# A mixture-of-experts layer: gate/up of two experts in four passes, and TensorE's order fixed to the program's

## Chip, cores, metric

One core of a Trainium2 chip runs the whole layer in one launch. The metric is the device time of one execution in microseconds. A core has TensorE (matmuls), VectorE, ScalarE, GpSimd and SyncE; SyncE issues the weight loads, and 16 DMA engines carry them.

## What is computed

A layer on 512 tokens of width 1024, all in float32: a mixer (mLSTM heads and pooling), then a mixture of 32 experts of which each token takes four, each time with a residual, and a last norm. The change lies in the experts:

```python
logits = xt @ w_router + b_router
top_vals, top_idx = lax.top_k(logits, 4)
top_gates = softmax(top_vals)
# for each expert e, on the tokens that chose it:
gate = minimum(xb @ w_gate[e] + b_gate[e], 7.0)
up = clip(xb @ w_up[e] + b_up[e], -7.0, 7.0)
y = (gate * sigmoid(1.702 * gate) * (up + 1.0)) @ w_down[e] + b_down[e]
# out[token] += top_gate * y
```

The three matrices of an expert are 1024 x 1024 floats, 4 MB each; the 32 experts have 384 MB together, and each is read once.

## The kernel before

The mixer and the router take the first 230 us or so; after them come the experts, which this document calls the expert stage.

**Tokens and blocks.** The tokens of an expert are gathered in blocks of 32, by GpSimd's indirect DMAs. A block is computed in four column quarters on the four 32-row groups of TensorE, so that gate and up of a block fill one PSUM bank (`gub[b]`, 128 x 512) and its down projection half a bank (`db[b]`; blocks 2 and 3 use `gub[2:]` for it). Each expert has room for four blocks. Blocks 0 and 1 are always computed, block 2 under `If(CR[e] > 64)` and block 3 in a second If inside it, `If(CR[e] > 96)`, on the count of tokens that TensorE reads into a register. Here expert 0 has three blocks, expert 1 and expert 2 two each; experts 29, 30 and 31 have three; two experts (9 and 25) have four; the others two or three. Where an If is not taken, TensorE jumps over its matmuls.

**Weights.** Gate and up of an expert come in four chunks of 2.1 MB (two DMAs, a quarter of gate and a quarter of up), down in two chunks of the same size (one DMA each): `load_chunks`, L121 to L145. A chunk goes into one of ten slots in turn (in the trace `wr`, `ym`, `wlo`, `whi`, by the buffer that the space came from). The order is gate/up of experts 0 and 1, down of 0, gate/up of 2, down of 1, gate/up of 3, and so on; so gate/up of expert 2 takes over the slots of gate/up of expert 0, down of 1 and the first half of gate/up of 3 those of expert 1, the second half of gate/up of 3 those of down of 0, and down of 2 and the first half of gate/up of 4 those of gate/up of 2. SyncE issues the loads in this order, each once the slot's last reader is through; eight DMAs can be under way.

**The work on a chunk.** `gu_mm` (L916 to L925) multiplies blocks by chunks; `each` (L891 to L903) cuts an expert's eight row groups into passes: in each pass blocks 0 and 1 over the pass's chunks, then block 2 under its If, then block 3. `GU_STEPS` gives the number of passes of an expert's gate/up: two for experts 0 and 1, four for 30 and 31, one for the others; down always has one pass, over both chunks (`d_mm`, L958 to L970). Ahead of each gate/up two small matmuls put the bias into `gb` (L912, called at L1133), ahead of each down projection into `yb`. VectorE takes gate/up out of PSUM (`act_blocks`, first at L931), ScalarE has the sigmoid, VectorE the products and the transposes for the down projection. Behind expert 0's gate/up the softmax of the gates runs (`softmax`, matmuls at L999).

**The order.** In the loop over `g["way"]` (L1123 on) the program writes the work expert by expert, but a scheduler may reorder each engine's instructions where dependencies allow. It also moves whole Ifs. `tc.manual_schedule` on an engine keeps the order of the program: before, for TensorE in expert 0's gate/up alone (`ME = (0,)`), and for four engines (`ENDM`) behind expert 30's down projection to the end.

Of the kernel before, what the change touches and what calls it, by code (L numbers as in the profile page):

```python
# [14 lines left out]
AF = mybir.ActivationFunctionType  # L15
# [9 lines left out]
NE = 32  # L25
# [12 lines left out]
RD = 2  # L38
ENDM = ("PE", "DVE", "Activation", "Pool")
HA = (False, False)  # L40
GU_STEPS = {0: 2, 1: 2, 30: 4, 31: 4, NE: 1}
D_STEPS = {NE: 1}
DBG = {}
CA = 2
PB = 2
MAN = ()
ME = (0,)


@with_exitstack  # L50
def tile_block(ctx, tc, x, norm1_g, w_in, ig_b, fg_b, conv_w, head_norm_g, pool_w, pool_scale,
# [111 lines left out]
    open_ring(RING, "right")  # L163
    mixer(tc, nc, ctx, g)
    moe(tc, nc, ctx, g)
    overflow(tc, nc, ctx, g)

# [670 lines left out]
def moe(tc, nc, ctx, g):  # L838
    pe, act, dve, gp, sp = nc.tensor, nc.scalar, nc.vector, nc.gpsimd, nc.sync
# [7 lines left out]
    with tc.tile_pool(name="mo", bufs=1) as mo, tc.tile_pool(name="mop", bufs=1, space=PSUM) as pp:  # L847
        gub = [pp.tile([128, 512], F32, name=f"gub{b}") for b in range(NB)]
        db = [pp.tile([128, 512], F32, name=f"db{b}") for b in range(2)] + gub[2:]
        gb = pp.tile([128, 512], F32, name="gb")  # L850
        yb = pp.tile([128, 512], F32, name="yb")[:, :256]
        gbs = mo.tile([128, 512], F32, name="gbs")
# [10 lines left out]
        def gather(e, between=None):  # L863
            gather_block(e, 0)
            i = gather_block(e, 1)
            if between:
                between()
            with tc.issue_after(i.ins):
                GR[e] = gp.value_load(cnt[0:1, e:e + 1], min_val=0, max_val=S)
            with tc.If(GR[e] > 64):  # L870
                gather_block(e, 2)
                with tc.If(GR[e] > 96):
                    gather_block(e, 3)
            if e == 0:
                g["rest"][0](1)

        def select(e):
            SEL[e] = mo.tile([128, 128], FR, name="sel", tag="sel", bufs=2)
            act.activation(SEL[e].rearrange("p (q i) -> p q i", q=4),
                           ident[:, 4 * e:4 * e + 4, None].to_broadcast([128, 4, 32]), AF.Copy)  # L880

        def xpose(e):
            XT[e] = []
            for b in range(NB):
                t = mo.tile([128, 256], F32, name=f"xt{b}", tag=f"xt{b}", bufs=2) if b < 3 else xgt[:, 4]
                i = dve.transpose(t, xg[b])  # L886
                if b:
                    tc.keep_in_program_order(i)
                XT[e].append(t)

        def each(e, mm, steps):  # L891

            for i in range(steps):
                cs = range(8 * i // steps, 8 * (i + 1) // steps)
                if e == NE - 1 and i == steps - 1:
                    for b in (2, 0, 1, 3):
                        some(e, mm, b, cs)
                    continue
                mm(e, (0, 1), cs)
                with tc.If(CR[e] > 64):  # L900
                    mm(e, (2,), cs)
                    with tc.If(CR[e] > 96):  # L902
                        mm(e, (3,), cs)  # L903

        def some(e, mm, b, cs):
            with tc.If(CR[e] > 32 * b) if b > 1 else ExitStack():
                mm(e, (b,), cs)

        def bias(e, ps, c0, c1, alone=True):
            with tc.issue_after(last[0]) if last and alone else ExitStack():  # L910
                for part in range(2):
                    i = pe.matmul(ps, SEL[e], par[:, part, c0:c1], start=(part == 0), stop=(part == 1 and alone))  # L912
            if not last:
                last[:] = [i.ins]
# [57 lines left out]
        def y_block(e, b):  # L972
            y = mo.tile([128, 256], F32, name="y", tag="sy", bufs=6)
            if e < NE - 1:
                dve.tensor_tensor(y, db[b][:, :256], ybs, op=OP.add)  # L975
            dve.tensor_scalar(y, y if e < NE - 1 else db[b][:, :256], gs[:, e * NB + b:e * NB + b + 1], None,  # L976
                              op0=OP.mult)
            return y
# [24 lines left out]
        def scatter_block(e, b, y):  # L1003
            i = gp.indirect_dma_start(out=yd, out_offset=bass.IndirectOffsetOnAxis(  # L1004
                ap=gi[:, e * NB + b:e * NB + b + 1], axis=0), in_=y, in_offset=None,
                bounds_check=S * 4 - 1, oob_is_err=False, compute_op=OP.add)
            for o in scat[4 * e:]:
                tc.declare_no_dep(i.ins, o.ins, reason="an expert's tokens differ")
            scat.append(i)

        def for_blocks(e, f):
            f(0)
            f(1)
            with tc.If(GR[e] > 64):
                f(2)
                with tc.If(GR[e] > 96):  # L1016
                    f(3)

        def finish_early():

            a, t2 = g["ring_tile"](), g["ring_tile"]()
            t2 = t2.rearrange("p a b -> p (a b)")
            nfb, nfq, yg, junk = t2[:, 0:1024], t2[:, 1024:1280], t2[:, 1280:2304], t2[:, 2304:3328]
            nf = g["normf_g"]
            act.dma_start(nfb, nf.partition_broadcast(128))
            for q in range(4):
                act.dma_start(nfq[q * 32:(q + 1) * 32, :], nf[q * 256:(q + 1) * 256].partition_broadcast(32))
            gp.memset(yg, 0.0)  # L1028

            quarters, qi = t2[:, 3328:3456], t2[:, 3456:3584].bitcast(I32)  # L1030
            gp.iota(qi, pattern=[[1, 128]], base=128, channel_multiplier=-1)
            dve.tensor_scalar(qi, qi, 31, None, op0=OP.bitwise_and)
            dve.tensor_scalar(quarters, qi, 0.0, None, op0=OP.is_equal)
            e = NE - 1

            def fetch(b):
                gp.indirect_dma_start(out=yg[:, b * 256:(b + 1) * 256], out_offset=None, in_=yd,  # L1037
                                      in_offset=bass.IndirectOffsetOnAxis(ap=gi[:, e * NB + b:e * NB + b + 1], axis=0),
                                      bounds_check=S * 4 - 1, oob_is_err=False)

            for_blocks(e, fetch)
            for t in range(NT):
                if t == RD:
                    g["final"][0](1)
                read(a, t)
            if RD == NT:
                g["final"][0](1)
            return dict(a=a, nfb=nfb, yg=yg, nfq=nfq, junk=junk, quarters=quarters, sums=t2[:, 3584:3600])

        def read(a, t):  # L1050
            sp.dma_start(a[:, t], yd[t * 512:(t + 1) * 512, :].rearrange("(p j) w -> p (j w)", j=4))
# [54 lines left out]
                todo[step[0]](int(step[1]))  # L1106

        CR, last = {}, []
        if MAN:
            ctx.enter_context(tc.manual_schedule(engines={getattr(mybir.EngineType, n) for n in MAN}))  # L1110
        def begin():
            for ps in gub[2:]:
                dve.memset(ps, 0.0)
# [5 lines left out]
        act.activation(gbs, gb, AF.Copy)  # L1119
        xpose(0)  # L1120
        g["order"].close()
        final = {}
        for kind, e in g["way"]:  # L1123
            if kind == "gu":
                with tc.issue_after(last[0]):
                    CR[e] = pe.value_load(cnt[0:1, e:e + 1], min_val=0, max_val=S)
                if e + 1 < NE:
                    gather(e + 1)
                    select(e + 1)
                    xpose(e + 1)  # L1130
                with tc.manual_schedule(engines={mybir.EngineType.PE}) if e in ME else ExitStack():
                    if e:
                        bias(e, gb, 0, 512)  # L1133
                        act.activation(gbs, gb, AF.Copy)  # L1134
                    each(e, gu_mm, GU_STEPS.get(e, GU_STEPS[NE]))
                load_chunks(4)
                if e == 0:
                    softmax()
                act_blocks(e)
                continue  # L1140
            if e < NE - 1:
                bias(e, yb, 512, 768)
                act.activation(ybs, yb, AF.Copy)
            if e < NE - 1:
                each(e, d_mm, D_STEPS.get(e, D_STEPS[NE]))
            load_chunks(2)
            if e < NE - 1:
                ys = [y_block(e, b) for b in range(NB)]
                for_blocks(e, lambda b: scatter_block(e, b, ys[b]))
            if e == NE - 2:  # L1150
                final = finish_early()
                end = ctx.enter_context(ExitStack())
                end.enter_context(tc.manual_schedule(engines={getattr(mybir.EngineType, n) for n in ENDM}))
        finish(**final)
# [134 lines left out]
```

## Time and profile before

| | us |
|---|---|
| median of three runs | 1288.06 |
| the three runs | 1287.28 to 1289.83 |
| profiled execution, its own time | 1292.79 |
| its span, first to last instruction | 1291.1 |
| TensorE busy | 1164.1 (90%) |
| VectorE busy | 577.9 (45%) |
| GpSimd busy | 262.2 (20%) |
| ScalarE busy | 218.8 (17%) |
| DMA, mean | 352 GB/s |
| mean granted TensorE clock | 0.964 |

Busy shares are averages over the whole span, and the stages differ: the first 230 us are the mixer, with a DMA load far below that of the experts. In the rows further down, a clock of 1.00 is the full granted TensorE clock (2.4 GHz) and 0.50 its lower level (1.2 GHz). A timeline row gives start and length in us, the engine (SPq is SyncE's queue, where an issue is no work of the engine), the line, what is written from what, the number of instructions (x32), and in brackets the idle time before it with what ended it. A float32 matmul of the program is two records in the trace. PEq with a line is TensorE's own sequencer at that line: at L900 the If around block 2, at L902 the one around block 3. "issue" is idle time for which the profile shows no wait.

### The profile page before, as it was taken

How to read it: one execution, taken by the hardware profiler on the slowest of the kernel's cores; microseconds unless marked ns; L12 is line 12 of the kernel's file. 1: busy time of each engine (PE TensorE's matmuls, PEld its weight loads, DVE VectorE, ACT ScalarE, POOL GpSimd, SP SyncE). 2: the span in 40 equal slices, each digit the busy share in tenths (PEclk: the TensorE clock that was granted, in tenths of full speed). 3: DMA queues.
4: the chain of work that ended last, by engine and by line, in shares of the span. 5: the costliest groups of instructions: out<-in, count | busy, mean ns of one | idle time of the engine just before them, and what ended most of it. 6: DMA issues, size and time to landing. Idle time of an engine off the chain costs nothing. (4 is left out here: it accounts for less than half of the span.)

```text
span 1291.1 us, 27952 instructions
## 1 busy us (share of the span) xinstructions
PE 1164.1 (90%) x11694; PEld 559.2 (43%) x11695; DVE 577.9 (45%) x1487; ACT 218.8 (17%) x434; POOL 262.2 (20%) x276
## 2 busy tenths in 40 slices
PE   8999999998988889999888899999888999989984
PEld 6788676333333334443333333434343434333432
DVE  4684655464444344434444444453524444444415
ACT  4693453110000000000000000010100000000002
POOL 2011022202211212113211121212121212120123
PEclk9999999998988999999988999999999999999997
DMA  8731766889999999999999999999999999999693
GB/s 326 255 106 39 234 230 224 315 331 397 406 410 410 413 411 409 410 404 394 402 410 413 417 400 409 402 408 401 405 404 398 403 396 400 387 411 394 217 341 151
DMA packets 86289, 454.98 MB, mean 352 GB/s; under 512 B 13857, under 2 KB 35089, under 8 KB 44762
## 3 DMA queue, kind: packets, MB, share of 16 engines
q1 hardware_dynamic: 67674, 428.58, 82.4%
q0 software_dynamic: 15408, 17.17, 6.0%
q10 hardware_dynamic: 3024, 6.55, 1.4%
q8 instruction: 143, 2.34, 0.7%
q14 instruction: 40, 0.33, 0.1%
HBM read 439.82 MB, written 16.92 MB: 354 GB/s over the span
## 5 line engine op out<-in xcount | busy, mean ns | idle before, releaser
L921 PE MATMUL gub<-wr,xt 128*32 128x512 f32 x3520 | 400.8, 603 | 24.0 <-PEq L900 10.3
L931 DVE TENSOR_TENSOR t<-gub,gbs 128x512 f32<-128x512 f32 x128 | 85.0, 685 | 423.9 <-PE gub L921 285.4
L921 PEld LDWEIGHTS gub<-wr,xt 128*32 128x32 f32 x3520 | 121.0, 111 | 286.4 <-issue 260.4
L858 POOL DMA_INDIRECT xgt<-h2d,gi x81 | 84.4, 1042 | 623.7 <-DVE xt L886 531.7
L966 PE MATMUL db<-wr,at 128*32 128x256 f32 x2944 | 183.1, 398 | 29.9 <-PEq L900 15.0
L1004 POOL DMA_INDIRECT yd<-y,gi x78 | 124.0, 1590 | 157.1 <-DVE y L976 136.9
L966 PEld LDWEIGHTS db<-wr,at 128*32 128x32 f32 x2944 | 105.1, 114 | 95.7 <-issue 29.0
L934 ACT ACTIVATE sg<-t 128x256 f32<-128x256 f32 x128 | 52.5, 415 | 531.9 <-DVE t L932 525.5
L975 DVE TENSOR_TENSOR y<-db,xgt 128x256 f32<-128x256 f32 x62 | 26.1, 421 | 156.8 <-PE db L966 156.7
L1134 ACT ACTIVATE gbs<-gb 128x512 f32<-128x512 f32 x31 | 18.6, 599 | 303.1 <-PE gb L912 294.8
L921 PE MATMUL gub<-whi,xt 128*32 128x512 f32 x528 | 62.4, 607 | 6.0 <-DMA whi<-in_w_up_dram 2.4
L921 PE MATMUL gub<-wlo,xt 128*32 128x512 f32 x528 | 62.8, 608 | 5.3 <-DMA wlo<-in_w_up_dram 3.9
L921 PE MATMUL gub<-ym,xt 128*32 128x512 f32 x480 | 57.3, 600 | 2.8 <-PEq L900 1.5
L941 DVE STREAM_TRANSPOSE at<-sg 128x256 f32<-128x256 f32 x96 | 58.9, 636 | 0.1
L1259 DVE SCALAR_TENSOR_TENSOR sg<-t,sg 128x256 f32<-128x256 f32 x128 | 50.9, 420 | 0.1
L1258 DVE TENSOR_TENSOR sg<-sg,t 128x256 f32<-128x256 f32 x128 | 49.0, 415 | 3.4 <-ACT sg L934 3.4
L976 DVE TENSOR_SCALAR y<-y,gs 128x256 f32<-128x256 f32 x124 | 49.4, 420 | 2.2
L214 DVE TENSOR_TENSOR wlo<-wraw,whi 128x1024 fp32r<-128x1024 f32 x30 | 36.7, 1223 | 28.5 <-ACT whi L213 28.4
L966 PE MATMUL gub<-wr,at 128*32 128x256 f32 x640 | 39.5, 393 | 6.1 <-PEq L902 5.0
L886 DVE STREAM_TRANSPOSE xt<-xgt 128x256 f32<-128x256 f32 x96 | 35.1, 411 | 14.2 <-PE gub L921 9.3
L921 PEld LDWEIGHTS gub<-whi,xt 128*32 128x32 f32 x528 | 19.7, 112 | 45.7 <-issue 41.4
L213 ACT ACTIVATE whi<-wraw 128x1024 fp32r<-128x1024 f32 x30 | 31.7, 1059 | 38.7 <-PE sc L267 11.0
(315 smaller groups left out, 1267.3 us busy)
## 6 DMA issues: line engine op xcount, KB each, us to landing
wr<-in_w_down_dram SPq DMA_DIRECT2D x45, 2048.0 KB, 23.7
wr<-in_w_gate_dram SPq DMA_DIRECT2D x89, 1024.0 KB, 12.4
wr<-in_w_up_dram SPq DMA_DIRECT2D x89, 1024.0 KB, 26.8
ym<-in_w_gate_dram SPq DMA_DIRECT2D x13, 1024.0 KB
ym<-in_w_up_dram SPq DMA_DIRECT2D x13, 1024.0 KB, 25.3
wlo<-in_w_gate_dram SPq DMA_DIRECT2D x13, 1024.0 KB
wlo<-in_w_up_dram SPq DMA_DIRECT2D x13, 1024.0 KB, 27.5
whi<-in_w_gate_dram SPq DMA_DIRECT2D x13, 1024.0 KB
```

Source lines behind the costliest of these rows:

```text
L214: low.tensor_tensor(l3, rv, h3.bitcast(F32), op=OP.subtract)
L858: return gp.indirect_dma_start(out=xg[b], out_offset=None, in_=h2d, in_offset=bass.IndirectOffsetOnAxis(ap=gi[:, e * NB + b:e * NB + b + 1 ...
L886: i = dve.transpose(t, xg[b])
L921: i = pe.matmul(gub[b][q * 32:(q + 1) * 32, :], XT[e][b][:, c * 32:(c + 1) * 32], w[:, :, c % 2, q * 256:(q + 1) * 256], start=(c == 0), s ...
L931: dve.tensor_tensor(t, gub[b], gbs, op=OP.add)
L934: act.activation(sg, t[:, 0:256], AF.Sigmoid, scale=ALPHA)
L941: dve.transpose(AT[e, b].rearrange("p (c s) -> p c s", c=8), sgs[b].rearrange("p (i c) -> p c i", c=8))
L966: i = pe.matmul(db[b][q * 32:(q + 1) * 32, :256], AT[e, b][:, c * 32:(c + 1) * 32], w[:, c % 4, q * 256:(q + 1) * 256], start=(c == 0 and ...
L976: dve.tensor_scalar(y, y if e < NE - 1 else db[b][:, :256], gs[:, e * NB + b:e * NB + b + 1], None, op0=OP.mult)
L1004: i = gp.indirect_dma_start(out=yd, out_offset=bass.IndirectOffsetOnAxis(ap=gi[:, e * NB + b:e * NB + b + 1], axis=0), in_=y, in_offset=No ...
L1258: dve.tensor_tensor(sg, sg, t[:, 0:256], op=OP.mult)
L1259: dve.scalar_tensor_tensor(sg, t[:, 256:], 1.0, sg, op0=OP.add, op1=OP.mult)
```

## The change

Experts 0 and 1 do their gate/up in four passes of one chunk each, where they had two passes of two chunks. And TensorE's order is no longer fixed for expert 0's gate/up alone, but from the head of the loop over the experts until expert 30's down projection; behind it `ENDM` takes over as before. The settings `MAN` and `ME` go.

```diff
--- before.py
+++ after.py
@@ -38,13 +38,11 @@
 RD = 2
 ENDM = ("PE", "DVE", "Activation", "Pool")
 HA = (False, False)
-GU_STEPS = {0: 2, 1: 2, 30: 4, 31: 4, NE: 1}
+GU_STEPS = {0: 4, 1: 4, 30: 4, 31: 4, NE: 1}
 D_STEPS = {NE: 1}
 DBG = {}
 CA = 2
 PB = 2
-MAN = ()
-ME = (0,)
 
 
 @with_exitstack
@@ -1106,8 +1104,6 @@
                 todo[step[0]](int(step[1]))
 
         CR, last = {}, []
-        if MAN:
-            ctx.enter_context(tc.manual_schedule(engines={getattr(mybir.EngineType, n) for n in MAN}))
         def begin():
             for ps in gub[2:]:
                 dve.memset(ps, 0.0)
@@ -1119,6 +1115,8 @@
         act.activation(gbs, gb, AF.Copy)
         xpose(0)
         g["order"].close()
+        order = ExitStack()
+        order.enter_context(tc.manual_schedule(engines={mybir.EngineType.PE}))
         final = {}
         for kind, e in g["way"]:
             if kind == "gu":
@@ -1128,11 +1126,10 @@
                     gather(e + 1)
                     select(e + 1)
                     xpose(e + 1)
-                with tc.manual_schedule(engines={mybir.EngineType.PE}) if e in ME else ExitStack():
-                    if e:
-                        bias(e, gb, 0, 512)
-                        act.activation(gbs, gb, AF.Copy)
-                    each(e, gu_mm, GU_STEPS.get(e, GU_STEPS[NE]))
+                if e:
+                    bias(e, gb, 0, 512)
+                    act.activation(gbs, gb, AF.Copy)
+                each(e, gu_mm, GU_STEPS.get(e, GU_STEPS[NE]))
                 load_chunks(4)
                 if e == 0:
                     softmax()
@@ -1149,6 +1146,7 @@
                 for_blocks(e, lambda b: scatter_block(e, b, ys[b]))
             if e == NE - 2:
                 final = finish_early()
+                order.close()
                 end = ctx.enter_context(ExitStack())
                 end.enter_context(tc.manual_schedule(engines={getattr(mybir.EngineType, n) for n in ENDM}))
         finish(**final)
```

What this does to TensorE's rows. First place: TensorE at the head of expert 1's gate/up (`gub_1996` to `gub_1999` are the banks of blocks 0 to 3; `wr_681`, `wr_1164`, `wr_1442` and `ym` its four chunks). Before:

```order
L912 MATMUL gb<-par,sel 128x512
L900 COMPARE_AND_BRANCH
L902 COMPARE_AND_BRANCH
L921 MATMUL gub_1999<-wr_681,xgt 32x512 x8
L921 MATMUL gub_1999<-wr_1164,xgt 32x512 x8
L902 UNCONDITIONAL_BRANCH x2
L921 MATMUL gub_1998<-wr_681,xt_2088 32x512 x8
L921 MATMUL gub_1998<-wr_1164,xt_2088 32x512 x8
L900 UNCONDITIONAL_BRANCH x2
L900 COMPARE_AND_BRANCH
```

And with the change:

```order
L910 MATMUL gb<-par,sel 128x512 x2
L919 MATMUL gub_1996<-wr_681,xt_2086 32x512 x4
L919 MATMUL gub_1997<-wr_681,xt_2088 32x512 x4
L919 MATMUL gub_1996<-wr_681,xt_2086 32x512 x4
L919 MATMUL gub_1997<-wr_681,xt_2088 32x512 x4
L898 COMPARE_AND_BRANCH
L919 MATMUL gub_1998<-wr_681,xt_2090 32x512 x8
L900 COMPARE_AND_BRANCH
L919 MATMUL gub_1999<-wr_681,xgt 32x512 x8
L900 UNCONDITIONAL_BRANCH x2
L898 UNCONDITIONAL_BRANCH
```

Before, both passes' Ifs stand between the two bias matmuls, ahead of blocks 0 and 1. With the change each chunk has its pass: blocks 0 and 1, then the If with blocks 2 and 3 of this chunk; three more passes of this form follow.

Second place: TensorE in expert 2's gate/up, one pass in either program (its chunks are `wr_2226` to `wr_2235` before, `wr_2229` to `wr_2238` now). Before, near its beginning:

```order
L921 MATMUL gub_1996<-wr_2226,xt_2413 32x512 x4
L921 MATMUL gub_1997<-wr_2226,xt_2415 32x512
L900 COMPARE_AND_BRANCH
L902 COMPARE_AND_BRANCH
L921 MATMUL gub_1999<-wr_2226,xgt 32x512 x8
L921 MATMUL gub_1999<-wr_2229,xgt 32x512 x8
L921 MATMUL gub_1999<-wr_2232,xgt 32x512 x8
L921 MATMUL gub_1999<-wr_2235,xgt 32x512 x8
L902 UNCONDITIONAL_BRANCH x2
L921 MATMUL gub_1998<-wr_2226,xt_2417 32x512 x8
L921 MATMUL gub_1998<-wr_2229,xt_2417 32x512 x8
L921 MATMUL gub_1998<-wr_2232,xt_2417 32x512 x8
```

And with the change, at its end:

```order
L919 MATMUL gub_1997<-wr_2238,xt_2418 32x512 x4
L919 MATMUL gub_1996<-wr_2238,xt_2416 32x512 x4
L919 MATMUL gub_1997<-wr_2238,xt_2418 32x512 x4
L898 COMPARE_AND_BRANCH
L919 MATMUL gub_1998<-wr_2229,xt_2420 32x512 x8
L919 MATMUL gub_1998<-wr_2232,xt_2420 32x512 x8
L919 MATMUL gub_1998<-wr_2235,xt_2420 32x512 x8
L919 MATMUL gub_1998<-wr_2238,xt_2420 32x512 x8
L900 COMPARE_AND_BRANCH
L919 MATMUL gub_1999<-wr_2229,xgt 32x512 x8
L919 MATMUL gub_1999<-wr_2232,xgt 32x512 x8
L919 MATMUL gub_1999<-wr_2235,xgt 32x512 x8
```

Before, the If stands behind the first five matmuls; the other blocks' matmuls on the four chunks follow it. With the change it stands behind blocks 0 and 1 of all four chunks, with the reads of the four chunks in it. Expert 0's down projection changes likewise: its If stood inside the gate/up of expert 1, and now stands behind both chunks of its own blocks 0 and 1.

## Rows read from the trace of the kernel before

**Rows 1.** Page, part 1: busy us (share of the span) x instructions of each engine.
```profile
PE 1164.1 (90%) x11694; PEld 559.2 (43%) x11695; DVE 577.9 (45%) x1487; ACT 218.8 (17%) x434; POOL 262.2 (20%) x276
```

**Rows 2.** DMA load by stretch: busy us (x instructions) per engine; PEclk, DMA share, GB/s at the end.
```profile
276.00:1175.00 899.00, 814.10 (x9060) 335.83 (x9054) 369.90 (x1007) 77.39 (x196) 186.56 (x142) 0.96 1.02 405
```

**Rows 3.** Chain that ended last, late in the stage: start us, us, what.
```profile
1126.20 26.84 DMA wr<-in_w_up_dram
1153.06 28.10 DMA wlo<-in_w_up_dram
```

**Rows 4.** Timeline of TensorE, late: start, us, line, out<-in, count, idle before and releaser.
```profile
1126.32 3.64 PE L921 MATMUL gub<-wlo,xt 128*32 128x512 f32 x32 [1.60 <-DMA wlo<-in_w_up_dram]
1132.34 3.64 PE L921 MATMUL gub<-whi,xt 128*32 128x512 f32 x32 [2.39 <-DMA whi<-in_w_up_dram]
...
1144.01 5.35 PE L966 MATMUL gub<-wr,at 128*32 128x256 f32 x64 [3.12 <-PEq L902]
...
1183.12 1.92 PE L966 MATMUL db<-ym,at 128*32 128x256 f32 x28 [1.97 <-issue]
```

**Rows 5.** DMA load by stretch around experts 0 to 2, columns as in rows 2.
```profile
239.00:243.00 4.00, 3.55 (x36) 0.94 (x32) 2.82 (x10) 0.00 (x0) 2.00 (x2) 1.00 0.41 86
243.00:263.00 20.00, 16.92 (x230) 6.63 (x226) 11.07 (x35) 2.03 (x5) 1.99 (x2) 0.93 1.00 412
263.00:268.00 5.00, 4.62 (x43) 1.30 (x37) 5.00 (x15) 0.82 (x2) 0.00 (x0) 0.94 0.44 131
268.00:273.00 5.00, 4.70 (x74) 2.61 (x69) 1.56 (x4) 0.00 (x0) 0.00 (x0) 1.00 0.89 374
273.00:276.00 3.00, 3.00 (x36) 1.21 (x32) 0.00 (x0) 0.00 (x0) 0.00 (x0) 1.00 0.42 87
```

**Rows 6.** SyncE's loads around experts 1 to 3, columns as in rows 4.
```profile
266.42 8.20 SPq L139 DMA_DIRECT2D wr<-in_w_down_dram  x2
...
288.65 0.33 SPq L136 DMA_DIRECT2D whi<-in_w_gate_dram  x1
...
301.67 5.26 SPq L139 DMA_DIRECT2D wr<-in_w_down_dram  x2
```

**Rows 7.** Timeline of TensorE, expert 0's gate/up in two passes.
```profile
230.51 10.51 PE L921 MATMUL gub<-wr,xt 128*32 128x512 f32 x96 [0.58 <-DVE xt L886]
241.48 10.51 PE L921 MATMUL gub<-wr,xt 128*32 128x512 f32 x96 [0.45 <-PEq L902]
```

**Rows 8.** Timeline of TensorE, one of the four passes of expert 30.
```profile
1197.59 5.36 PE L921 MATMUL gub<-wr,xt 128*32 128x512 f32 x48 [0.37 <-PEq L902]
```

**Rows 9.** Timeline of VectorE, expert 0's gate/up taken out of PSUM.
```profile
258.25 1.28 DVE L931 TENSOR_TENSOR t<-gub,gbs 128x512 f32<-128x512 f32 x2
```

**Rows 10.** Stretches before and after TensorE's rest ahead of expert 1, columns as in rows 2.
```profile
256.70:260.15 3.45, 0.95 (x6) 0.43 (x10) 3.45 (x13) 0.82 (x2) 0.00 (x0) 1.00 1.02 425
260.15:263.56 3.41, 3.41 (x21) 0.86 (x24) 3.41 (x10) 1.21 (x3) 0.00 (x0) 0.50 1.00 413
```

**Rows 11.** Timeline of TensorE, two blocks of two chunks one behind the other.
```profile
701.89 3.64 PE L921 MATMUL gub<-wlo,xt 128*32 128x512 f32 x32
705.35 3.62 PE L921 MATMUL gub<-whi,xt 128*32 128x512 f32 x32
```

**Rows 12.** TensorE's waits, whole span: us in total, times, longest us.
```profile
PE gub L921 <- PEq L900: 12.1, 13, 3.3
...
PE gub L921 <- PEq L902: 5.6, 17, 0.7
PE gub L921 <- issue: 5.1, 4, 2.3
```

**Rows 13.** Timeline of TensorE, expert 0's down projection, and a jump of expert 2.
```profile
269.72 1.93 PE L966 MATMUL gub<-wlo,at 128*32 128x256 f32 x32 [0.30 <-DVE xgt L941]
...
281.47 3.66 PE L966 MATMUL db<-wlo,at 128*32 128x256 f32 x64
...
294.36 3.55 PE L921 MATMUL gub<-wr,xt 128*32 128x512 f32 x16 [3.28 <-PEq L900]
```

## Prediction

> **What bounds the kernel now.** I read the page's shares first, then the load of the DMA engines by stretch, then the chain of waits that ended last, and only then TensorE's own waits. TensorE is busy 90% of the span [rows 1], which looks like the bound. But from 276 to 1175 us the DMA engines are full, with a share of 1.02 and 405 GB/s [rows 2], while TensorE idles for 85 of those 899 us. The chain of waits consists, over this stretch, of weight transfers one behind the other, each some 27 us from issue to landing [rows 3]. Late in the stage TensorE stands still until a landing: 1.60 us at 1126.32 and 2.39 us at 1132.34 [rows 4]. So it has no lead that could soak up a later stream: a microsecond that the weight stream loses early arrives at the end as a microsecond, and idle time of TensorE in the middle is free unless it delays a load.
>
> The stream is not full everywhere. Between 239 and 276 us there are three holes [rows 5]. Measured by bytes against the 412 GB/s of the full stretch 243 to 263, they are (1 - 86/412) x 4 = 3.2 us, (1 - 131/412) x 5 + (1 - 374/412) x 5 = 3.9 us and (1 - 87/412) x 3 = 2.4 us, together 9.5 us. Each ends when SyncE may issue the next load [rows 6]; the bytes follow the issue by about 1.5 us (an estimate from rows 5 and 6: a load issued at 266.42, full speed only after 268). What holds each load is the slot it wants: ten slots, and a chunk takes the slot of the chunk ten places ahead once TensorE's last reader is through. Here, around experts 0 to 2, TensorE does set when the stream moves. So the question is when TensorE releases slots between 236 and 310 us.
>
> **The change part by part.** I replay TensorE from 230.51, where expert 0's first pass starts [rows 7]. A chunk of 2.10 MB takes 2.10/0.412 = 5.1 us of the stream.
>
> Expert 0 in four passes of three blocks: 4 x 5.36 + 3 x 0.45 = 22.8 us by the pass of expert 30, which has this form [rows 8], and by the 0.45 us gap in front of a new pass [rows 7]. It ends at 253.3 rather than 252.0, a loss of 1.3. But expert 2's chunks are now let go one by one, at 236.0, 241.8, 247.6 and 253.5, where two passes gave two behind each. The stream then runs from 239.2 to 260.1 with 0.5 us missing: the first hole, 3.2 us, closes.
>
> The softmax matmuls and VectorE's work behind them move by the same 1.3 us. VectorE frees the first PSUM bank of expert 1 with its add of 258.25, 0.64 us long [rows 9]; 1.3 later that is 260.2, and this is when expert 1 starts, as before. TensorE's idle time ahead of it is now about 2.3 us. Before, 3.45 us with 0.95 busy were followed by 3.41 us at half the granted clock [rows 10], the 1.2 GHz level, which costs 1.7 us. Whether a shorter rest still brings it no row shows: between 0 and 1.7 I take half, 0.85.
>
> Expert 1 has two blocks, so both Ifs are skipped. In program order a pass takes 3.62 us to its last matmul's end (3.46 where the next pass follows at once) [rows 11], and behind each of the four stands a skipped If, at which TensorE drains and jumps; a slot is free only behind it. For its price s I have [rows 12]: 5.6 us over 17 jumps past the fourth block (0.33 each, down to quarter bodies), 12.1 + 5.1 us over 13 jumps past the third (1.3 each), and 3.3 at most. Expert 1's bodies are a quarter of a whole one, so I take 0.5, nearer the first; ends 0.33 and 1.3. With 3.62 + 0.5 for a pass and the 0.85 in the first, the four slots come free at 265.2, 269.3, 273.4 and 277.5. Then yb's bias, 0.5, and expert 0's down projection, now both chunks of two blocks first and the third block last: 2 x 3.66 + 2 x 1.93 = 11.2 us [rows 13] and 0.6 for its Ifs, to 289.8. Its two slots come free there together; before, the second was loaded again at 288.65 [rows 6] and the first a chunk earlier. Expert 2 (two blocks): gb 0.7, 4 x 3.46 = 13.9, and one If skipped at its end, past a whole body, s' = 1.3 (0.33 to 3.3), hence 305.7. All four of its slots wait for that, since the program keeps the skipped body's reads of all four chunks behind the last pass; before, they went one by one from 301.67.
>
> Stream after, by issue plus 1.5 us: d(1) starts at 266.8 instead of at 260.1 (hole 6.7); four chunks run to 287.3; the next starts at 291.3 (hole 4.0); two chunks to 301.5; then 307.2 (hole 5.7). With the 0.5 that is 16.9 us of holes against 9.5: **the stream is 7.4 us later.** Lower end: s and s' at 0.33, no slow clock, bytes 1.0 behind an issue: 7.4 - 0.7 - 1.0 - 0.85 - 1.5 = +3.3. Upper end: s = 1.3, s' = 3.3, 1.7 of slow clock: 7.4 + 3.2 + 2.0 + 0.85 = +13.4.
>
> The Runtime: NRT & Kernel Launch page of the Trainium skill (Instruction fetch mechanics) says that a taken branch whose target lies outside the pages held must fetch its page by DMA before the engine goes on. By that rule the short jumps of expert 1 would mostly stay inside and cost the least, which alone would make the sum +6.7, and a long jump costs a fetch; the trace agrees in that the same kind of jump takes 0.33 us or ten times that.
>
> Experts 3 to 29: the If body moves from behind three chunks to behind four. The work behind the last landing is the same sum in another order, so nothing. Four slots released together come up to 3 x 3.46 = 10.4 us later than one by one. Cover: 27 us in flight at 405 GB/s are 10.9 MB, some 5.2 of the ten slots [rows 2, 3]; the other 4.8 hold 25 us of stream. If that cover were gone, each expert would cost microseconds. Skipped Ifs of the down projection stall TensorE as before, beside the stream: nothing.
>
> End: experts 29 to 31 take block 2, so only order changes, and GpSimd's memset still stands in front of expert 29's scatters and still waits for the last reader of that expert's down weights. I take 0.
>
> Sum: +7.4 on the profiled execution's 1292.79 would be 1300.2. That execution is itself 4.7 above the median of the three runs, 1288.06, and I forecast against the median: 1288.06 + 7.4, about **1295 us**.
>
> **The rivals.** *No measurable difference, about 1290.* TensorE loses 5.1 us in two stalls near the end, 3.12 us in front of the 64 matmuls at 1144.01 and 1.97 at 1183.12 [rows 4]. If these jumps are cheap in the new order, TensorE arrives 5.1 us sooner at expert 30 and the sum is +2.3. For: such stalls vary from expert to expert, from 0.33 to 3.3 us [rows 12]. Against: with the stream 7 us late, expert 30's chunks may not be there yet.
>
> *Faster, about 1285.* The slots come free chunk by chunk even so: the loads of expert 0's two down slots and of expert 2's four don't wait for the Ifs at the end, because nothing of a skipped body holds them. Expert 0's first down slot is then free at 277.5 + 0.5 + 3.7 = 281.7 and its second at 285.4, expert 2's first at 294 and so on each 3.5 us, always ahead of the stream; of the holes 0.5 + 6.7 remain, and 2.3 us are won, 3.2 if the slow clock stays away. It is decided by whether those loads are issued ahead of 288 and of 301. For: in the order before, they were. Against: there the If stood ahead of the last chunk and bound nothing; now its readers of every chunk stand behind the last pass.
>
> *Much slower, about 1308.* Each of the five jumps costs as much as the longest, 3.28 at 294.36 [rows 13]: 4 x 2.8 + 2.0 = 13 on top of 7.4. Against: the short jumps of experts 0 and 30 never did. A milder form of it is a stream that starves once more in the middle, at an expert with four blocks, about 1300. That the change would not do what it says, the order rules out: in both places TensorE's rows stand as the program writes them.
>
> **How the numbers follow.** The forecast has 0.56; no difference 0.21; faster 0.14; much slower or starving later 0.09. A measurement of this kernel can tell 0.2%, 2.6 us, from no change. Faster by more is then 0.14, within it 0.21, slower 0.65. The sum's own ends give 1291 to 1301; to hold 8 in 10 the range reaches towards the faster case and part of the slower one: 1284 to 1304.
>
> **What would show it.** Right: no hole near 240; a hole of 6 to 7 us between 260 and 268; both loads into expert 0's down slots issued together near 290, four loads together near 306, each behind a hole; later the same 405 GB/s and the waits for landings near 1126 shifted by about 7. Wrong: expert 2's four loads issued before 301, or TensorE reaching expert 1 before 258 us, or waits for landings gone near the end; or a new hole after 310.

## The result and the profile after

The changed kernel takes 1296.63 us (median of five runs, 1294.81 to 1299.0) beside 1289.13 us for the kernel before on the same chip (1287.28 to 1292.31): a ratio of 1.0069, 95% interval 1.0053 to 1.0085, so 7 to 11 us slower. A second series, further down, gave 1.0079 (1.0064 to 1.0095). The profiled execution took 1299.0 us, its span is 1297.2 us, 6.1 us more than the span before.

The number is the predicted one. The way to it is not: the forecast looked for these microseconds in the weight stream around experts 0 to 2, and they arise at the other end of the expert stage. The load of the DMA engines by stretch (busy us and count for each engine, then TensorE's granted clock, DMA share, GB/s), answering to [rows 5] and [rows 2]:

```profile
239.00:243.00 4.00, 3.55 (x36) 0.94 (x32) 3.05 (x11) 0.00 (x0) 1.99 (x2) 1.00 1.02 424
243.00:261.00 18.00, 15.40 (x230) 6.09 (x226) 7.16 (x23) 0.82 (x2) 1.99 (x2) 1.00 1.00 384
261.00:267.00 6.00, 5.82 (x56) 1.78 (x60) 6.00 (x17) 1.21 (x3) 0.00 (x0) 1.00 0.48 165
...
271.00:275.00 4.00, 3.83 (x40) 1.21 (x36) 0.00 (x0) 0.00 (x0) 0.00 (x0) 1.00 0.96 352
...
286.00:290.00 4.00, 2.80 (x38) 1.10 (x30) 2.58 (x8) 0.60 (x1) 2.90 (x2) 1.00 0.73 246
...
300.00:306.00 6.00, 5.32 (x70) 2.17 (x66) 2.79 (x8) 1.40 (x4) 1.04 (x1) 1.00 0.45 128
...
276.00:1175.00 899.00, 801.39 (x9056) 315.04 (x9060) 364.98 (x1008) 78.52 (x196) 186.61 (x142) 0.96 1.01 403
```

The hole near 240 is gone (424 GB/s where there were 86), and three stand where they were foreseen. But they are short. By bytes against 412 GB/s they are (1 - 165/412) x 6 = 3.6, 1.6 and 4.1 us, with 1.2 between 243 and 261 and 0.6 between 271 and 275: 11.1 us, where 16.9 were forecast and before there were 9.5. Over one and the same window, 239 to 310 us, the stream has 350 GB/s before and 346 now, which is 0.7 us (1.2 us in the second profiles further down, 358 and 351 GB/s). SyncE's loads answer to [rows 6]:

```profile
264.70 4.14 SPq L137 DMA_DIRECT2D wr<-in_w_down_dram  x2
...
287.28 0.33 SPq L134 DMA_DIRECT2D wlo<-in_w_gate_dram  x1
...
288.18 0.38 SPq L134 DMA_DIRECT2D whi<-in_w_gate_dram  x1
...
303.58 0.81 SPq L137 DMA_DIRECT2D wr<-in_w_down_dram  x2
...
1178.54 10.56 SPq L137 DMA_DIRECT2D wr<-in_w_down_dram  x4
```

The pattern is as foreseen: both of expert 0's down slots are loaded again together, and expert 2's slots too, in a burst. The last row is expert 29's down projection, near the end of the stream: issued at 1178.54, and in the profile before at 1178.75; in the middle of the stage, expert 13's is issued at 651.43, and before at 651.27. **The stream is not late at all when it ends.** TensorE, which answers to [rows 7] and [rows 4], shows where the time is (start, us, line, what, count, idle before and its releaser):

```profile
260.91 3.64 PE L919 MATMUL gub<-wr,xt 128*32 128x512 f32 x32 [1.35 <-DVE t L929]
264.73 3.64 PE L919 MATMUL gub<-wr,xt 128*32 128x512 f32 x32 [0.18 <-PEq L898]
...
1164.83 12.20 PE L919 MATMUL gub<-wr,xt 128*32 128x512 f32 x96 [2.79 <-DMA wr<-in_w_up_dram]
...
1181.38 3.64 PE L964 MATMUL db<-ym,at 128*32 128x256 f32 x64
1190.70 1.21 PE L910 MATMUL gb<-par,sel 128*128 128x512 f32 x2 [5.68 <-PEq L898]
1191.85 7.40 PE L919 MATMUL gub<-wlo,xt 128*32 128x512 f32 x48
...
1199.82 5.36 PE L919 MATMUL gub<-whi,xt 128*32 128x512 f32 x48 [0.57 <-PEq L900]
```

The first two rows are expert 1's first passes: full clock, and 0.18 us for a skipped If. The third is expert 29's last stretch of gate/up, 12.20 us where the second profile of this kernel, further down, has 10.51: 1.7 us of slow clock that belong to this execution, the slowest of the five. The others lie between expert 28's down projection (two blocks, its If is skipped) and expert 30's gate/up: TensorE idles for 5.68 us at the skipped If, and the pass behind it takes 7.40 us where the next takes 5.36. The window over it has the clock:

```profile
1190.70:1199.20 8.50, 8.50 (x50) 2.20 (x50) 0.90 (x3) 0.60 (x1) 1.55 (x1) 0.69 1.03 399
```

A granted clock of 0.69 on average is a part at 1.2 GHz and the rest at 2.4. Idle time and slow clock make 5.68 + 0.5 (the bias, 1.21 for 0.7) + 2.0 = 8.2 us; before, the same If had 2.2 us, a stall of 1.97 [rows 4] and 0.18 ahead of it.

### The profile page after: what moved, and what is told of

The parts are those of the page before. It is cut to its first block, busy times and chain, and to the rows that moved or that the text cites. A ratio compares the mean times of both kernels' runs of the same rounds, so it can differ in the third digit from the quotient of the medians.

```text
span 1297.2 us, 27999 instructions
## 1 busy us (share of the span) xinstructions
PE 1152.2 (89%) x11694; PEld 534.9 (41%) x11695; DVE 571.1 (44%) x1487; ACT 220.0 (17%) x434; POOL 261.8 (20%) x276
## 3 DMA queue, kind: packets, MB, share of 16 engines
q8 instruction: 143, 2.34, 0.7%
## 5 line engine op out<-in xcount | busy, mean ns | idle before, releaser
L919 PE MATMUL gub<-wr,xt 128*32 128x512 f32 x3520 | 412.3, 621 | 17.7 <-DMA wr<-in_w_up_dram 11.8
L919 PEld LDWEIGHTS gub<-wr,xt 128*32 128x32 f32 x3520 | 117.8, 114 | 297.3 <-issue 276.0
L964 PE MATMUL db<-wr,at 128*32 128x256 f32 x2944 | 166.3, 380 | 2.9 <-DMA wr<-in_w_down_dram 2.0
L964 PEld LDWEIGHTS db<-wr,at 128*32 128x32 f32 x2944 | 93.4, 110 | 66.0 <-DMA wr<-in_w_down_dram 2.2
L877 ACT ACTIVATE sel<-ident 128x128 fp32r<-128x128 f32 x32 | 9.8, 308 | 590.8 <-PE yb L910 582.9
L910 PE MATMUL gb<-par,sel 128*128 128x512 f32 x64 | 27.2, 511 | 69.3 <-PEq L898 52.5
L919 PE MATMUL gub<-wlo,xt 128*32 128x512 f32 x528 | 68.2, 645 | 2.5 <-issue 2.0
L910 PEld LDWEIGHTS gb<-par,sel 128*128 128x128 f32 x64 | 11.1, 218 | 84.6 <-issue 84.6
L974 DVE TENSOR_SCALAR y<-y,gs 128x256 f32<-128x256 f32 x124 | 43.4, 373 | 1.9
L973 DVE TENSOR_TENSOR y<-gub,xgt 128x256 f32<-128x256 f32 x62 | 25.6, 418 | 35.1 <-PE gub L964 18.5
```

What stands on the lines that cost most here:

```text
L919: i = pe.matmul(gub[b][q * 32:(q + 1) * 32, :], XT[e][b][:, c * 32:(c + 1) * 32], w[:, :, c % 2, q * 256:(q + 1) * 256], start=(c == 0), s ...
L964: i = pe.matmul(db[b][q * 32:(q + 1) * 32, :256], AT[e, b][:, c * 32:(c + 1) * 32], w[:, c % 4, q * 256:(q + 1) * 256], start=(c == 0 and ...
```

## The experiments

Two theories at first. **Start**: the prediction's own, a stream 7 us late from experts 0 to 2 on. **End**: the time arises on TensorE between expert 28's down projection and expert 30. All ratios are to the kernel before, run beside each experiment on the same chip (its medians there are 1287.0, 1287.2 and 1286.7 us), each with its 95% interval.

**Order free again at the end.** In the changed kernel, ahead of expert 28's down projection:

```diff
         for kind, e in g["way"]:
+            if (kind, e) == ("d", NE - 4):
+                order.close()
```

> The changed kernel, but TensorE's order is given back to the scheduler ahead of expert 28's down projection, so that this If (not taken) stands between the two down chunks again, as before. Theory 'end' (the 7.5 us arise on TensorE between expert 28's down projection and expert 30's gate/up, where the changed kernel idles 5.68 us at the skipped If and then runs expert 30's first pass in 7.40 instead of 5.36 us): about 1289 us, the time of before, with expert 30 starting near 1186. Theory 'start' (the weight stream is late from experts 0 to 2 on, as the prediction has it): 1296 us as in the changed kernel.

Measured: 1295.17 us, ratio 1.0062 (1.0044 to 1.0081). The number is that of "start", but not its cause: the stream was again about where the first profile before has it (expert 29's down issued at 1179.07), and TensorE stalled at the same If in its old place, between the two down chunks:

```profile
1182.72 3.65 PE L964 MATMUL db<-ym,at 128*32 128x256 f32 x60 [2.36 <-PEq L898]
1188.29 0.62 PE L964 MATMUL db<-ym,at 128*32 128x256 f32 x4 [1.92 <-issue]
```

That is 4.3 us for the jump that had 2.2 in the kernel before, at the same place of the program, so "end" holds only in part: it foresaw the price of before. So the place of the If alone doesn't set its price. The pass behind it ran at full clock here, and beside the second profile of the kernel before (below), whose stream is 2.4 us earlier, the 4.3 us are only part of this run's 8; the rest isn't explained.

**Order fixed at the end only.** The kernel before, with

```diff
+        order = ExitStack()
...
+            if (kind, e) == ("d", NE - 4):
+                order.enter_context(tc.manual_schedule(engines={mybir.EngineType.PE}))
...
                 final = finish_early()
+                order.close()
```

> The kernel before, with TensorE's order fixed to the program's only from expert 28's down projection to expert 30's. Theory 'end': 1295 to 1297 us, with an idle time of 4 to 6 us ahead of expert 30's gate/up. Theory 'start': 1289 us, no change.

Measured: 1290.88 us, ratio 1.0028 (1.0014 to 1.0041): less than half of the changed kernel's loss, and below the forecast of "end". The stall is there, 3.97 us, and the slow pass, in a profiled execution (1293.44) that was slower than the median:

```profile
1184.78 1.21 PE L912 MATMUL gb<-par,sel 128*128 128x512 f32 x2 [3.97 <-PEq L900]
1185.93 7.79 PE L921 MATMUL gub<-wlo,xt 128*32 128x512 f32 x48
```

**Two passes again.** `GU_STEPS = {0: 2, 1: 2, ...}` in the changed kernel.

> The changed kernel with experts 0 and 1 in two passes again, order fixed. Theory 'end': 1296 us as in the changed kernel, since the stream's start doesn't set the end. Theory 'start': expert 2's chunks are freed by twos again and the hole near 240 is back, so 3 us later than the changed kernel, about 1299 us.

Measured: 1292.96 us, ratio 1.0049 (1.0032 to 1.0067). Below both forecasts, though the hole near 240 was back (90 GB/s from 238 to 240), and "start" wanted it slower than the changed kernel. The stall ahead of expert 30 was another one again: 0.91 us at the If and 2.63 a few matmuls later.

**The start alone.** The changed kernel with `order.close()` ahead of expert 1's down projection.

> The changed kernel with TensorE's order given back to the scheduler from expert 1's down projection on: the change around experts 0 to 2 alone. Theory 'start': 1296 us. Theory 'end': within 1.5 us of 1289, since the holes of the stream around experts 0 to 2 are 10 us long in both traces, by their bytes.

Measured: 1288.89 us, ratio 1.0011 (0.9999 to 1.0023): no difference that shows. That is the end of theory "start". What remained open was whether the fixed order of experts 3 to 27 costs time in its own right ("middle"), or the jump ahead of expert 30 ("jump").

**Without the jump.** In `each`, for the down projection of expert 28 alone:

```diff
                 mm(e, (0, 1), cs)
+                if e == NE - 4 and mm is d_mm:
+                    continue
                 with tc.If(CR[e] > 64):
```

> The changed kernel without the Ifs of expert 28's down projection: its third and fourth block's down matmuls are left out (this input doesn't take them), and with them the jump. Theory 'jump' (TensorE's skipped If ahead of expert 30 and the slow clock behind it cost the time): no idle time of several us ahead of expert 30's gate/up, its first pass 5.4 us instead of 7.4, and 5 to 7 us less than the changed kernel, so 0 to 3 us above the kernel before. Theory 'middle' (the fixed order of experts 3 to 27 costs time by a later stream): as the changed kernel, 6 to 8 us above the kernel before.

Measured: 1287.09 us, ratio 1.0006 (0.9995 to 1.0018). With the whole change in it but for one expert's Ifs that aren't taken, the kernel is as fast as before, and "middle" falls. (The edit takes the skipped bodies' code out as well, so what lies behind them moves; from expert 30's first pass to 1250 us neither this trace nor the changed kernel's second one shows an idle time of TensorE above 1.2 us.) TensorE goes from the down projection to expert 30 without an idle row, and the first pass takes 5.36:

```profile
1163.65 10.51 PE L921 MATMUL gub<-wr,xt 128*32 128x512 f32 x96 [2.55 <-DMA wr<-in_w_up_dram]
...
1182.08 0.73 PE L912 MATMUL gb<-par,sel 128*128 128x512 f32 x2
1182.74 5.36 PE L921 MATMUL gub<-wlo,xt 128*32 128x512 f32 x48
```

**Both kernels a second time.** The kernel before and the changed kernel, unchanged, for second profiles.

> The kernel before, unchanged: a second profile of it. Ratio 1.000 within 0.15%. If its stall at expert 28's skipped If is the same (about 2.2 us, expert 30 starting some 22 us after the landing of expert 29's last chunk), the stall belongs to the program; if it differs by several us, it varies from run to run. Both theories expect holes of 8 to 10 us around experts 0 to 2 and no hole from 330 to 1175 us.

> The changed kernel, unchanged: a second profile. If the stall ahead of expert 30 belongs to the code it is 5.5 to 5.9 us again with the slow clock behind it; if it varies from run to run, anything from 0.9 to 5.7. The weight stream at expert 29's down chunks within 3 us of the kernel before.

Measured: the kernel before 1288.42 us, ratio 0.9997 (0.9985 to 1.0009), its stall at expert 28 the same as in its first profile, 2.08 and 0.18 us. The changed kernel 1296.32 us, ratio 1.0079 (1.0064 to 1.0095), its stall 6.25 after 5.68, a little above the 5.9 expected: it belongs to the program, not to the run. In these two profiles the streams end nearly alike (expert 29's down issued at 1176.69 and 1176.10), so they can be laid beside each other. First before, then changed:

```profile
1161.89 10.51 PE L921 MATMUL gub<-wr,xt 128*32 128x512 f32 x96 [0.18 <-PEq L902]
...
1181.03 1.92 PE L966 MATMUL db<-ym,at 128*32 128x256 f32 x28 [2.08 <-issue]
1182.88 0.73 PE L912 MATMUL gb<-par,sel 128*128 128x512 f32 x2
1184.09 5.36 PE L921 MATMUL gub<-wlo,xt 128*32 128x512 f32 x48 [0.47 <-DMA wr<-in_w_down_dram]
1189.78 5.36 PE L921 MATMUL gub<-whi,xt 128*32 128x512 f32 x48 [0.33 <-PEq L902]
```

```profile
1162.35 10.51 PE L919 MATMUL gub<-wr,xt 128*32 128x512 f32 x96 [2.63 <-DMA wr<-in_w_up_dram]
...
1173.73 3.66 PE L964 MATMUL db<-wr,at 128*32 128x256 f32 x64
...
1187.10 1.22 PE L910 MATMUL gb<-par,sel 128*128 128x512 f32 x2 [6.25 <-PEq L898]
1188.24 7.06 PE L919 MATMUL gub<-wlo,xt 128*32 128x512 f32 x48
1195.88 5.36 PE L919 MATMUL gub<-whi,xt 128*32 128x512 f32 x48 [0.57 <-DMA wr<-in_w_down_dram]
```

| TensorE reaches | before | changed | later by |
|---|---|---|---|
| the last 96 records of expert 29's gate/up | 1161.89 | 1162.35 | 0.5 |
| expert 30's first pass | 1184.09 | 1188.24 | 4.2 |
| its second pass | 1189.78 | 1195.88 | 6.1 |
| end of the span | 1287.1 | 1293.5 | 6.4 |

Of the 6.4 us, 5.6 arise between the first row and the third: the stall and the slow clock behind it.

**Short bodies.** `D_STEPS = {28: 4, NE: 1}` in the changed kernel.

> The changed kernel with expert 28's down projection in four passes, so that each skipped body is a quarter as long. Theory 'jump', if long bodies make it dear: four jumps of 0.2 us each (as measured behind expert 1's four passes, 0.17 each) instead of one of 5.7, no slow clock behind, 4 to 6 us less than the changed kernel. If a jump costs the same whatever it skips: 2 to 3 us each, 3 us or more above the changed kernel. Theory 'middle': no change against the changed kernel.

Measured: 1296.19 us, ratio 1.0068 (1.0055 to 1.0082), no gain; the number is that of "middle", which the run without the jump rules out. The profiled execution (1293.28) was the fastest of its six. Three of the four jumps cost little (the last 0.96 with the read of a register in it), but one cost 2.69 us, and slow clock followed it (32 records in 2.47 and 2.92 us, 1.93 ahead of it):

```profile
1176.38 1.93 PE L964 MATMUL db<-wr,at 128*32 128x256 f32 x32 [0.18 <-PEq L898]
1181.01 2.47 PE L964 MATMUL db<-ym,at 128*32 128x256 f32 x32 [2.69 <-PEq L898]
1183.63 2.92 PE L964 MATMUL db<-ym,at 128*32 128x256 f32 x32 [0.16 <-PEq L898]
1187.51 0.73 PE L910 MATMUL gb<-par,sel 128*128 128x512 f32 x2 [0.96 <-PEq L898]
```

So neither the place of the If nor the length of its body decides alone. What is left to try is where the code lies. The view of the DMA queues (packets, MB, share of 16 engines), cut to the stall of the changed kernel (1186 to 1190), shows one transfer on the queue of instructions:

```profile
q1 hardware_dynamic: 125, 1.72, 101.4%
q8 instruction: 1, 0.02, 1.5%
```

It has 16 KB (143 such transfers have 2.34 MB over the whole span) and shares the 16 engines with a weight stream that takes 101% of them. In the kernel without the jump no such transfer lies between 1180 and 1184, around the start of expert 30. One such transfer in 4 us proves little by itself, as they come every 6 to 15 us here; what it has to do with the stall is taken up behind the next experiment.

**Code shifted, by matmuls that do nothing.** The changed kernel, in front of expert 15's bias, once with 32 and once with 64:

```diff
+                if e == 15:
+                    for _ in range(32):
+                        pe.matmul(gb[:, 0:8], SEL[e], par[:, 0, 0:8], start=True, stop=True)
```

> The changed kernel with 32 tiny matmuls (8 columns, into the bias bank before its bias) in front of expert 15's gate/up: they cost 2 to 3 us of TensorE where it idles beside the weight stream, and shift the code of everything behind by a quarter of one of the 16 KB code transfers of the trace (if a matmul is two instructions of 64 bytes). Theory 'code' (the long stall is a wait for a code transfer, and its length depends on where in the code the skipped body lies): another idle time ahead of expert 30 than 5.7 us, anywhere from 0.9 to 5, and the time 0 to 7 us below the changed kernel's. Theory 'place' (it belongs to the If at the end of the down projection): 5 to 6 us again, and the time of the changed kernel.

> The same with 64 tiny matmuls, half a code transfer. Theory 'code': again another stall ahead of expert 30, different from the run with 32; of the two and the changed kernel at least one lies at 3 us or less, with a time at least 3 us below the longest. Theory 'place': 5 to 6 us in all three.

Measured: with 32, 1296.66 us, ratio 1.0077 (1.0061 to 1.0093); **with 64, 1289.94 us, ratio 1.0024 (1.0013 to 1.0035).** Sixty-four useless matmuls more, and the kernel is some 6 us faster than the changed one. With 64 TensorE comes to expert 28's down projection when the changed kernel does (1173.82, and 1173.73 in its second profile); the stall ahead of expert 30 is 2.15 us, the clock stays up, and expert 30's second pass starts 6.2 us earlier (1189.67 for 1195.88) in a span that is 6.5 us shorter:

```profile
1173.82 3.66 PE L964 MATMUL db<-wr,at 128*32 128x256 f32 x64
...
1183.08 0.73 PE L910 MATMUL gb<-par,sel 128*128 128x512 f32 x2 [2.15 <-PEq L898]
1183.74 5.36 PE L919 MATMUL gub<-wlo,xt 128*32 128x512 f32 x48
1189.67 5.36 PE L919 MATMUL gub<-whi,xt 128*32 128x512 f32 x48 [0.57 <-PEq L900]
```

With 32 the time is that of the changed kernel, the upper end of what "code" allowed. The stall ahead of expert 30 is 3.28, the pass behind is slow, and another stall of 5.03 us has appeared two experts earlier, at expert 26's skipped If, where the changed kernel has 0.91 and the one with 64 has 3.64:

```profile
1124.94 1.22 PE L910 MATMUL gb<-par,sel 128*128 128x512 f32 x2 [5.03 <-PEq L898]
...
1189.92 0.72 PE L910 MATMUL gb<-par,sel 128*128 128x512 f32 x2 [3.28 <-PEq L898]
1190.57 7.05 PE L919 MATMUL gub<-wlo,xt 128*32 128x512 f32 x48
```

Theory "place" falls. How the stall hangs together with the code transfers, their times in the traces show (us; idle from the end of the last matmul of expert 28's down projection, and the transfer on the queue of instructions that ended last before TensorE went on):

| | idle from | code transfer | next matmul | behind the transfer's end |
|---|---|---|---|---|
| changed | 1185.02 | 1187.45 to 1188.39 | 1190.70 | 2.3 |
| changed, second profile | 1180.84 | 1183.79 to 1184.76 | 1187.10 | 2.3 |
| order fixed at the end only | 1180.81 | 1181.39 to 1182.45 | 1184.78 | 2.3 |
| 32 matmuls | 1186.64 | 1186.55 to 1187.61 | 1189.92 | 2.3 |
| 64 matmuls | 1180.93 | 1179.68 to 1180.78 | 1183.08 | 2.3 |

The stall ends 2.3 us behind the transfer each time, whether it lasts 2.15 or 6.25 us. It holds for the whole stage: of 117 idle times above 1.9 us ahead of a gate/up bias, in all fourteen traces from 280 to 1240 us, 106 end 2.1 to 2.7 us behind such a transfer. (In the kernel before, where a matmul of the down projection follows and no register is read first, it is 1.3 and 1.5.) By these times TensorE waits there for code, and the price of the jump goes with when the transfer starts: 1.25 us ahead of the idle time with 64 matmuls, 2.4 and 2.9 us into it in the changed kernel. The queue's count goes with TensorE's code, 143 transfers in the changed kernel, 144 with 64 matmuls more, 142 without the bodies.

Theory "code" stands. The Trainium skill says it in Runtime: NRT & Kernel Launch (Instruction fetch mechanics): code comes in 16 KB blocks by the sequencer's own DMA, in sequence, and a taken branch out of the blocks held waits for a fetch. The traces agree with the 16 KB and with the wait; they don't show which block a jump wanted, nor why its transfer starts early or late.

**A faster version.** Experts 0 to 2 in four passes, expert 0's down in two, so that each slot comes free behind its own pass; TensorE's order fixed for that stretch alone and again for expert 28's down, in four passes:

```diff
-GU_STEPS = {0: 4, 1: 4, 30: 4, 31: 4, NE: 1}
-D_STEPS = {NE: 1}
+GU_STEPS = {0: 4, 1: 4, 2: 4, 30: 4, 31: 4, NE: 1}
+D_STEPS = {0: 2, 28: 4, NE: 1}
...
+            if (kind, e) in (("d", 1), ("gu", NE - 2)):
+                order.close()
+            if (kind, e) == ("d", NE - 4):
+                order.enter_context(tc.manual_schedule(engines={mybir.EngineType.PE}))
```

> An attempt at a faster version: experts 0, 1 and 2 in four passes of gate/up, expert 0's down in two, order fixed up to expert 2's gate/up so that each chunk's slot comes free behind its own pass, the scheduler's order from there on, and expert 28's down in four passes in fixed order. Theory 'jump' with the stream's holes counted by bytes: the holes near 287 and 303 (1.1 and 3.3 us) close, the one near 263 stays, and the end has neither long jump nor slow clock: 3 to 6 us below the kernel before. Theory 'middle': 3 to 4 us below the kernel before from the holes alone.

Measured: 1283.28 us, ratio 0.9968 (0.9955 to 0.9982), faster than both. Of the holes the one near 263 is left; the others are full (416 and 415 GB/s):

```profile
260.00:266.00 6.00, 5.82 (x60) 1.80 (x56) 5.74 (x17) 1.21 (x3) 0.00 (x0) 1.00 0.40 135
...
284.00:290.00 6.00, 4.64 (x65) 2.96 (x60) 3.65 (x11) 0.60 (x1) 3.09 (x2) 1.00 1.01 416
...
298.00:306.00 8.00, 7.51 (x75) 2.69 (x68) 1.86 (x5) 0.58 (x2) 1.04 (x1) 1.00 1.05 415
```

Expert 29's down is issued at 1172.18, where the two profiles of the kernel before have 1178.75 and 1176.69, and the end follows: here a stream ahead of time does count, as the prediction's first part had it. (Two things changed at once, the holes and expert 28's jumps; TensorE is 6.3 us ahead of the second profile before already at expert 29's last 96 records, 1155.55 for 1161.89, and 7.1 at the end of the span.) A last one moved the softmax from behind expert 0's gate/up to behind expert 1's (`if e == 1:` in place of `if e == 0:`).

> The faster version with the softmax of the gates moved from behind expert 0's gate/up to behind expert 1's, so that expert 1's first pass starts some 4 us earlier and frees its slot earlier. By the holes of the stream: the one near 262 (3.8 us) shrinks to 0 to 1, and the kernel is 2 to 4 us below the faster version, about 6 to 8 us below the kernel before. If TensorE's work behind expert 29 sets the end by itself and not the stream, 0 to 1 us.

Measured: 1282.88 us, ratio 0.9969 (0.9955 to 0.9983): nothing on top. Its hole near 260 shrank, but the stream had 364 GB/s from 276 to 310, where the faster version has 407, and expert 29's down was issued at 1172.26, as without the move.

## Why the prediction was right, and where it was not

**The time and its sign**: 1295 forecast, 1296.6 measured, within 1284 to 1304. Two of its terms were wrong by 6 to 8 us each, one up and one down. That they cancel is luck, and the agreement is no support for the sum.

**What bounds the kernel**: right for most of the stage. The DMA engines are full from 306 us on in both (405 GB/s before and 403 now over 276 to 1175, the holes up to 306 included), and the version with shorter holes has its stream ahead and is faster. But the bound holds only while stream is left: from expert 28's down projection on TensorE sets the end.

**The hole near 240 closes**: right, 3.2 us. **Loads bunched behind the Ifs of expert 0's down and of expert 2**: right, at 287.28 and 288.18, and at 303.58.

**"The stream is 7.4 us later"**: wrong, the step that failed first. By bytes the holes grew by 1.6 us, 11.1 for 9.5 (0.7 to 1.2 over one window in both), not by 7.4: the first had 3.6 us where 6.7 were forecast, the second 1.6 for 4.0, the third 4.1 for 5.7. The price s of a short skipped If was 0.17 to 0.18, not 0.5, and no slow clock came behind the softmax (the clock is 1.00 from 261 to 267): d(1)'s load went out at 264.70. Expert 0's down let go 2.5 us ahead of the forecast, expert 2 2.1 us. And the stream ahead of the first hole ran at 384 GB/s, not 412, so it lasted longer and left less of a hole. Whatever there was of the 1.6 us no longer shows at 651 us, nor at 1178. The run of the start alone gives 1.0011 (0.9999 to 1.0023), 0 to 3 us at most.

**"End: I take 0"**: wrong, and this is where the time went. Between the two second profiles 5.6 of 6.4 us arise from expert 29's last matmuls to expert 30's second pass: a jump at 6.25 us for 2.3, and a slow pass. The step took the price of expert 28's skipped If for unchanged; in the new order TensorE waits longer for the code behind it (the table of code transfers above), and no transfer of weights is left that would cover the wait. The run without the jump shows it by its time, 1287.09, at 1.0006 of the kernel before, and the run with 64 matmuls by the same jump made cheap.

**"Skipped Ifs of the down projection stall TensorE as before, beside the stream: nothing"**: right for the middle, where the stream doesn't feel them (406 and 407 GB/s from 310 to 1100 us), though their sum is larger now (20.7 + 21.5 us before, 52.5 us now with the read of the register in it); wrong for expert 28, behind which no stream is left to cover it: from expert 30's first pass to 1250 us TensorE has no idle time above 1.2 us in the changed kernel's second profile. The waits, in us in total, times and longest, first before and then now:

```profile
PE db L966 <- issue: 21.5, 8, 4.3
PE db L966 <- PEq L900: 20.7, 14, 4.9
```

```profile
PE gb L910 <- PEq L898: 52.5, 17, 5.7
PE gb L910 <- issue: 15.6, 12, 2.9
```

**"The same sum in another order"** for the third block: nearly. TensorE now waits 2.63 us for expert 29's last chunk, where before it worked on the third block meanwhile; that is the 0.5 us of the table.

**The rivals**: the one without a difference had its finger on the right two rows, [rows 4], as stalls that "vary from expert to expert", but only as a gain. That the same jump can become dearer with code that was merely moved, and wake the slow clock, was in none of them. "Much slower" had the right kind of price at the wrong Ifs.

**What stays open**: which block of code each jump waits for, why its transfer starts when it does, and how far one would have to shift the code to make expert 28's jump cheap for good. Two shifts were tried, both into the middle of the stage. What made the run with 32 matmuls slow was not tested by itself: beside the one with 64 its TensorE is 5.7 us late already at expert 28's down projection (1179.52 for 1173.82), behind stalls of 5.03 and 3.64 us at expert 26, and 8.6 us late at expert 30's second pass. Which idle times bring the slow clock stays open too.

## What to carry to other kernels

An If that isn't taken isn't free: 0.2 to 6 us here, by when the next block of code comes, and a change that moves code can throw these dice again. So look for the last such jump behind which no transfer is left to hide it, and compare that stretch first when a reordering changes the time. And a forecast that hits the number is tested by its steps all the same: a run with the start alone and one without a single If cost little, and they moved the cause from one end of the expert stage to the other.

## What the runs showed that was not expected

- The same skipped If took 2.15 to 2.3 us (before), 5.7 to 6.3 (changed), 4.3 (order free at the end), 4.0 (order fixed at the end only), 3.3 and 2.15 (code shifted).
- Behind idle times of 5.68, 6.25, 3.97 and 3.28 us ahead of expert 30 its first pass took 7.1 to 7.8 us for 5.36, at an average granted clock of 0.66 to 0.78 over bias and pass; behind 2.15 us it ran at full clock. In between it goes either way: behind an idle time of 2.69 us (short bodies) the clock was 0.69, behind 2.79 and 2.55 us waiting for a landing 0.86 (changed) and 0.88 (two passes again), and behind 2.63 and 2.55 us of the same wait full (changed, second profile, and without the jump).
- The first matmul of an expert that follows an If body often waits some 1.15 us with no releaser, where TensorE reads the expert's count into a register just ahead of it. The changed kernel has twelve such waits, 15.6 us; before, where matmuls mostly stood between the If and that read, there are three, 2.0 us.
